# A trunk layer on one core: the output projection in seven block products for all tokens, adds moved to accumulating transfers, and norm one's scale and offset put on after the transposes

## The chip, the core and the metric

The kernel runs on one core of a Trainium2 chip. That core has TensorE (PE, matmuls into PSUM; PEld is its weight load), VectorE (DVE), ScalarE (ACT), GpSimd (POOL) and SyncE (SP), and 16 DMA engines. The metric is the device time of one execution in microseconds; the result of a kernel is the median over its runs.

## The reference

One post-norm transformer layer for 1024 tokens of width 1024, all in float32:

```python
h = x @ w_in                                     # q, k, v of branches A and B, two gates
y_a = chunk_band_attention(...) @ w_proj_a       # softmax over a band
y_b = stick_breaking_attention(...) @ w_proj_b
mix = (sigmoid(ga + b_gate_a) * y_a + sigmoid(gb + b_gate_b) * y_b) @ w_out
x = layer_norm(ALPHA * x + mix, ln1_g, ln1_b)
g, u = split(x @ w_ffn_in)
x = layer_norm(ALPHA * x + (silu(g) * u) @ w_ffn_out, ln2_g, ln2_b)
```

ALPHA is 2 to the power 0.25. The change touches everything from the gated projection of branch B to the FFN's second matmul.

## The kernel before

A float32 product of two matrices is computed from operands that are each split into a high and a low part in a matmul type (`split`, lines 109 and 110: ACT casts the high part, DVE subtracts to get the low one); one product is three matmuls (high by high, high by low, low by high), each 128 x 128 by 512. Large products are cut into two by two blocks and computed in the Winograd form: seven block products p = 1 to 7 over sums of blocks instead of eight.

The work is one long program; a scheduler puts each engine's instructions into an order from the order in which the code is written, and `keep_in_program_order` holds single ones in place. Within an engine instructions run in that order, so one that waits holds all behind it. Transfers are issued by SP and wait in its order as well; POOL issues none. Buffers come from pools by tag (`op`, `xt`, `kp`, `bw`, `gt`, `pt`, `yt`, and `qs`, `kh`, `kl`, `v` as a ring); a tile waits for the last use of the tile that had its slot. PSUM banks have tags too (`mm`, `sc`, `tr`, `pv`); the transposes use `tr`, of which there are three.

The stages around the change:

- Branch B's projection runs over eight channel blocks c, in the order 6, 7, 5, 4, 2, 3, 1, 0, in two token halves each. DVE multiplies the product by the gate gB and adds branch A's part mA (line 1146), which gives the merged branch m.
- The output projection takes m (as weights, 128 tokens at a time) and w_out. For the half of the tokens it goes by seven products, two token tiles each, 12 matmuls for each (line 1369); for token tiles 4 to 7 it goes plainly, in two column halves of 24 matmuls (lines 116 to 119). `take_in` (line 1348) adds each to ALPHA * x in `acc` on DVE.
- Norm one: DVE takes statistics (line 1183) and aggregates (1186), POOL raises the variance to the power -1/2 (1187), and DVE applies mean and scale g (1188), then 1/std and offset b (1191), over 128 x 1024.
- `x1_operands` transposes x1 in 128 x 128 pieces on PE (1209), ACT copies them out of PSUM (1219 for the first token half, 1229 for the second), and they are split; DVE forms the block sums that the FFN's seven products need (1247 to 1250).
- The FFN's first block of columns f = 0 goes plainly (`plain_half`), the 21 others in seven products (`run_pairs`, line 179). Their left sums `sl` are stored, and FFN-out (line 1512) loads them back; x1 is stored in `x_dr` and reloaded into `x` (line 1444), and `take_down` adds each FFN-out product to it on DVE (lines 1486 and 1489).

A product of the output projection, as it is written before:

```python
        for j in range(2):
            accs = by if p in (2, 5, 3) else bx
            ...
            take_in(t0 + j, cs, accs[j], scale)
            if p in (3, 4):
                norm_1(t0 + j)
```

## Time and profile before

| what | value |
|---|---|
| three runs | 1412.02, 1413.35, 1412.03 us (median 1412.03) |
| profiled execution | 1412.51 us, its span 1410.7 us |
| granted TensorE clock, mean | 0.999 |
| PE | 1399.7 us, 99% of the span, 6642 matmuls |
| DVE | 1034.1 us, 73%, 1671 instructions |
| ACT | 699.0 us, 50%, 1245 instructions |
| POOL | 236.0 us, 17%, 308 instructions |
| DMA | 292.28 MB, mean 207 GB/s |

Times in views are microseconds from the span's start. A row of the timeline or of the chain has start, length, engine, line, operation, output <- inputs, shapes and a count; in brackets stands how long the engine was idle before it and what released it. A row of groups has the count, the busy time and the mean in ns, and the idle time before. Rows on a transfer give how many, their size and the time from issue to landing.

### The profile page before, as it was taken

The page shows a single profiled execution, that of the slowest core. Times are in us where ns is not written, and L with a number is a line of the kernel's source. Part 1 is how long each engine was busy: PE and PEld are TensorE (multiplying, and loading weights), DVE is VectorE, ACT ScalarE, POOL GpSimd, SP SyncE. Part 2 cuts the span into 40 slices and gives each one's busy share as a digit, 9 for nine tenths or more (in the row PEclk, how much of TensorE's full clock was granted, in tenths as well). Part 3 has the DMA queues.
Part 4 walks back from the last instruction along what each step waited for, and adds up shares of the span by engine and source line. Part 5 has one row for each costly group of instructions (what it writes and reads, how often), then busy time and mean ns, then how long its engine had stood idle before and what let it go on. Part 6 is the DMA issues. An engine that isn't in the chain of part 4 may idle for free.

```text
span 1410.7 us, 18935 instructions
## 1 busy us (share of the span) xinstructions
PE 1399.7 (99%) x6642; PEld 1164.6 (83%) x6642; DVE 1034.1 (73%) x1671; ACT 699.0 (50%) x1245; POOL 236.0 (17%) x308
## 2 busy tenths in 40 slices
PE   9999999999999999999999999999999999999997
PEld 7888888888888888888888888888888888888886
DVE  8967657545887788878998967767677765847666
ACT  6544444545888888774413644434444443322220
POOL 0000000002555878750001000000000000000033
PEclk9999999999999999999999999999999999999999
DMA  7476468856676478755651144433444349996652
GB/s 254 165 286 224 178 236 303 295 179 238 212 231 208 130 252 281 253 198 194 231 202 75 61 148 166 149 141 143 164 164 149 143 144 342 411 385 236 233 194 90
DMA packets 98927, 292.28 MB, mean 207 GB/s; under 512 B 9728, under 2 KB 26112, under 8 KB 98832
## 3 DMA queue, kind: packets, MB, share of 16 engines
q1 hardware_dynamic: 98832, 291.07, 58.2%
q8 instruction: 52, 0.85, 0.3%
q14 instruction: 43, 0.35, 0.1%
HBM read 187.20 MB, written 100.17 MB: 204 GB/s over the span
## 4 chain that ended last, share of the span: by engine, by line
PE 94%; DVE 2%; DMA 1%; ACT 1%; issue 1%; POOL 0%; DVEq 0%; SPq 0%; ACTq 0%; POOLq 0%
PE sxf L179 16%; PE d L1512 15%; PE sxp L179 9%; PE szf L179 8%; PE v L481 5%; PE gps L606 4%; PE szp L179 4%; PE syf L179 4%; PE yAps L910 3%; PE ops L1369 3%; PE syp L179 2%; PE tp_b L817 2%; PE tp_a L817 2%; PE plain L347 1%; PE pv_b L833 1%; PE pv_b L832 1%
## 5 line engine op out<-in xcount | busy, mean ns | idle before, releaser
L1512 PE MATMUL d<-wd,sl 128*128 128x512 f32 (+1 forms) x924 | 207.7, 387 | 0.0
L1512 PEld LDWEIGHTS d<-wd,sl 128*128 128x128 f32 x924 | 172.3, 188 | 35.4
L1532 POOL TENSOR_TENSOR mv<-mv,neghalf 128x1 f32<-128x1 f32 x8 | 9.0, 1121 | 606.7 <-DVE mv L1531 606.7
L109 ACT CAST wd<-wd 128x512 fp32r<-128x512 f32 x77 | 45.9, 621 | 114.1 <-PE d L1512 66.8
L794 POOL TENSOR_TENSOR w_b<-w_b,kp_b 128x511 f32<-128x511 f32 (+3 forms) x96 | 96.0, 1012 | 23.2 <-DVE kp_b L789 16.7
L110 DVE TENSOR_TENSOR sl<-h,sl 128x512 fp32r<-128x512 f32 x77 | 52.6, 686 | 27.6 <-ACT sl L109 27.6
L789 DVE TENSOR_TENSOR_SCAN kp_b<-kp_b,ident_ps 128x512 f32<-128x512 f32 (+2 forms) x64 | 56.5, 885 | 21.0 <-ACT kp_b L786 20.0
L109 ACT CAST sl<-h 128x512 fp32r<-128x512 f32 x77 | 47.5, 620 | 48.1 <-PE syf L179 18.3
L1489 DVE TENSOR_TENSOR x<-d,x 128x512 f32<-128x512 f32 (+1 forms) x41 | 27.6, 675 | 47.6 <-PE d L1512 47.5
L786 ACT ACTIVATE kp_b<-sc_b 128x512 f32<-128x512 f32 (+3 forms) x96 | 48.3, 504 | 28.0 <-PE sc_b L706 23.6
L110 DVE TENSOR_TENSOR wd<-wd,wd 128x512 fp32r<-128x512 f32 x77 | 52.7, 709 | 10.7 <-ACT wd L109 10.6
L179 PE MATMUL szf<-x1S63h,wcf 128*128 128x512 f32 x168 | 55.1, 389 | 0.0
L110 DVE TENSOR_TENSOR pt_b<-tp_b,pt_b 128x512 fp32r<-128x512 f32 (+1 forms) x96 | 49.9, 544 | 6.6 <-ACT pt_b L109 5.7
...
L109 ACT CAST pt_b<-tp_b 128x512 fp32r<-128x512 f32 (+1 forms) x96 | 46.6, 503 | 8.0 <-PE tp_b L817 7.6
L759 POOL TENSOR_SCALAR w_a<-w_a,st_a 128x640 f32<-128x640 f32 (+2 forms) x64 | 42.2, 669 | 48.0 <-PE sc_a L706 26.6
L754 ACT ACTIVATE w_a<-w_a,st_a 128x640 f32<-128x640 f32 (+2 forms) x64 | 44.7, 700 | 8.6 <-DVE st_a L748 7.5
L787 ACT ACTIVATE w_b<-sc_b 128x511 f32<-128x511 f32 (+3 forms) x96 | 48.3, 504 | 0.0
L817 PE MATMUL tp_b<-ident,w_b 128*128 128x128 f32 x288 | 47.3, 272 | 0.2
L110 DVE TENSOR_TENSOR pt_a<-tp_a,pt_a 128x512 fp32r<-128x512 f32 (+1 forms) x96 | 44.6, 486 | 3.3 <-ACT pt_a L109 2.2
L1307 ACT ACTIVATE h<-sxf 128x512 f32<-128x512 f32 x21 | 12.6, 598 | 68.2 <-PE sxf L179 68.2
L817 PEld LDWEIGHTS tp_b<-ident,w_b 128*128 128x128 f32 x288 | 36.4, 140 | 11.1 <-DVE pt_b L110 1.1
...
## 6 DMA issues: line engine op xcount, KB each, us to landing
s_dr<-sl SPq DMA_DIRECT2D x77, 512.0 KB, 2.6
sl<-s_dr SPq DMA_DIRECT2D x77, 512.0 KB, 7.6
wLf<-in_w_ffn_in_dram SPq DMA_DIRECT2D x22, 512.0 KB, 4.3
wRf<-in_w_ffn_in_dram SPq DMA_DIRECT2D x22, 512.0 KB, 3.6
wd<-in_w_ffn_out_dram SPq DMA_DIRECT2D x22, 512.0 KB, 8.2
v_dr<-vc SPq DMA_DIRECT2D x16, 512.0 KB, 3.4
qs<-q_dr SPq DMA_DIRECT2D x16, 512.0 KB, 6.7
kh<-k_dr SPq DMA_DIRECT2D x16, 512.0 KB, 6.5
```

The lines of the kernel that those rows point to most:

```text
L109: return (nc.scalar.copy(dst_h, src), nc.vector.tensor_tensor(dst_l, src, dst_h.bitcast(F32), ALU.subtract))
L110: nc.vector.tensor_tensor(dst_l, src, dst_h.bitcast(F32), ALU.subtract))
L179: mm(acc, lw[:, ks], rx, start=(first and kt == i == 0), stop=(kt == 3 and i == 2), skip_group_check=not first)
L481: mm(accs[j], a, b, start=(first and kt == n == 0), stop=(kt == 3 and n == 2), skip_group_check=True)
L606: mm(acc[hf], lw[:, ks], rx[k][:, (LO, HI)[hf]], start=(k == j == 0), stop=(k == KT - 1 and j == 2))
L754: nc.scalar.activation(s[:, 0:w], s[:, 0:w], AF.Exp, bias=st[:, m:m + 1], scale=-1.0, accum_out=st[:, 2:3])
L786: nc.scalar.activation(kp[:, c0:e], sc[:, 0:n], AF.Sigmoid, scale=-1.0)
L787: nc.scalar.activation(be[:, m0:e], sc[:, m0 - c0:n], AF.Sigmoid)
L789: nc.vector.tensor_tensor_scan(kp[:, 0:e], kp[:, 0:e], ident_ps()[:, 0:e], 0.0, ALU.mult, ALU.add)
L794: nc.gpsimd.tensor_tensor(be[:, m0:e], be[:, m0:e], kp[:, m0 - 1:e - 1], ALU.mult)
L817: ins = tr(tp[:, (qb - lo_q) * P:(qb - lo_q + 1) * P], wt[qb - q0][:, (kb - qb) * P:(kb - qb + 1) * P], ident)
L1512: mm(part, a, b, start=(fresh and i == k == 0), stop=(i == n - 1 and k == 2), skip_group_check=not fresh)
```

## The change

*The output projection.* All eight token tiles go by seven products, four tiles each, in the order 1, 2, 5, 3, 6, then 7 and 4 interleaved by tile. That is 336 matmuls instead of 360. Products 1, 5 and 3 are evicted by ACT with 1/ALPHA, and x is added to them by a transfer that POOL issues and that accumulates into the tile; products 2, 6, 7 and 4 are added by DVE with 1/ALPHA. The norm is taken of x + mix/ALPHA, with EPS divided by ALPHA squared.

*Branch sums.* Branch A's part, and the left block sums `sum_1` and `sum_2`, are added by accumulating transfers from POOL. `sum_3` and `sum_4` stay on DVE. The left operands are split per product (`m_split`).

*Norm one.* POOL computes -mean/std with one more instruction, and ACT applies 1/std and it over 128 x 1024. Scale and offset are put on when x1 is evicted after its transposes, by columns of `gb_1`. `x_dr` keeps the norm without them; in FFN-out DVE multiplies by g (`scale_acc`), and POOL issues accumulating transfers that add b (`offset_acc`). `take_down` uses 1/ALPHA everywhere.

*Order.* Instructions of these stages are tied into lanes: "s" on ACT, "v" on DVE, "p" for POOL's transfers. FFN operands of f = 1 are formed during branch B, stored to DRAM by POOL and loaded back; those of f = 0 are loaded and split during the output projection. The sums of x1 are formed in two parts, later than before.

In counts: DVE has about 30 instructions fewer and ACT 20 more; POOL issues 45 transfers, where before it issued none.

```diff
+    lanes = dict(s=last_y[:1], v=last_y[1:])
+    def tied(lane, ins):
+        for before in lanes.get(lane, ()):
+            tc.add_manual_dep(ins.ins, before.ins.name, mybir.DependencyInfo(
+                mybir.DependencyClass.NoSync, mybir.DependencyReason.DATA), reason="lane")
+        lanes[lane] = [ins]
+        return ins
+    def halve(dst_h, dst_l, src):
+        hi, lo = split(dst_h, dst_l, src)
+        chain_s(hi)
+        chain(lo)
+    def plus(dst, src):
+        tied("p", nc.gpsimd.dma_start(dst, src, accum_op=ALU.add))
...
+    def sum_1(kt):
+        plus(m_raw[kt + 4][:, HI], m_raw[kt][:, HI])
+    def sum_2(kt):
+        plus(m_raw[kt][:, HI], m_raw[kt + 4][:, LO])
...
-            nc.vector.tensor_tensor(mA[:, cs], gB[:, cs], mA[:, cs], ALU.add)
+            chain(put(gB[:, cs], acc, gB[:, cs], ALU.mult))
+            if c < 2:
+                plus(gB[:, cs], m_dr[c][:, cs])
...
+    def statistics(name, n, tie=lambda ins: ins):
+        mv = sml.tile([P, 4], F32, name=f"mv{name}", tag="mv")
+        tie(nc.vector.bn_aggr(mv[:, 0:2], marks[name][:, 0:6 * n]))
         nc.gpsimd.tensor_tensor(mv[:, 2:3], mv[:, 1:2], neghalf, ALU.pow)
-        nc.vector.scalar_tensor_tensor(t, t, mv[:, 0:1], g, ALU.subtract, ALU.mult)
...
+    def scaled(dst, src, k):
+        chain_s(nc.scalar.activation(dst, src, AF.Identity, bias=gb_1[:, 8 + k:9 + k],
+                                     scale=gb_1[:, k:k + 1]))
...
+    def norm_1(tt):
+        mv, t = statistics(f"1_{tt}", 2, chain), acc_t[tt]
+        nc.gpsimd.tensor_scalar(mv[:, 3:4], mv[:, 0:1], mv[:, 2:3], -1.0, ALU.mult, ALU.mult)
+        chain_s(nc.scalar.activation(t, t, AF.Identity, bias=mv[:, 3:4], scale=mv[:, 2:3]))
...
+        if p in (1, 5, 3):
+            chain_s(nc.scalar.activation(t, accs[j], AF.Copy, scale=1 / ALPHA))
+            plus(t, x_rows(tt, cs))
+        else:
+            chain(nc.vector.scalar_tensor_tensor(t, accs[j], 1 / ALPHA, t, ALU.mult, ALU.add))
...
+    for n, (p, j) in enumerate(((7, 0), (7, 1), (4, 0), (7, 2), (4, 1), (7, 3), (4, 2), (4, 3))):
+        project_out(p, j)
+        if p == 4:
+            norm_1(j + 4)
+        if n > 3:
+            x1_operands(0, acc_t, (n - 4,))
...
+    def scale_acc(tts, cs):
+        for t in (acc_t[tt][:, cs] for tt in tts):
+            nc.vector.tensor_tensor(t, t, g1[:, cs], ALU.mult)
+    def offset_acc(tt):
+        nc.gpsimd.dma_start(acc_t[tt], bass.AP(tensor=ln1_b.tensor, offset=ln1_b.offset,
+                                               ap=[[0, P], [1, D]]), accum_op=ALU.add)
...
+    g1 = bcast(ln1_g, slot("xt", "ln1g"))
     load_acc(range(4))
+    scale_acc(range(4), LO)
```

Three places show how instructions move; a row has the line, the operation, output <- inputs, the shape, and in brackets the semaphores that it waits for. The first is ACT's order around the first evictions of x1 (`x1ps` are the transposed banks, `x1raw` their copies, `x1A` the operands, `acc` a token tile, `mv` its statistics). Before:

```order
L1219 COPY x1raw_7736<-x1ps_0_7726 128x512 [waits PE_49]
L1219 COPY x1raw_7736<-x1ps_4_7731 128x512 [waits PE_49]
L109 CAST x1A_0_7737<-x1raw_7736 128x512 [waits Activation_49]
L109 CAST x1A_0_7741<-x1raw_7736 128x512 [waits Activation_49]
L1219 COPY x1raw_7791<-x1ps_1_7781 128x512 [waits PE_49]
L1219 COPY x1raw_7791<-x1ps_5_7786 128x512 [waits PE_49]
L109 CAST x1A_1_7792<-x1raw_7791 128x512 [waits Activation_49]
L109 CAST x1A_1_7796<-x1raw_7791 128x512 [waits Activation_49]
```
Afterwards:

```order
L1399 ACTIVATE acc_7416<-acc_7416,mv_5_7787 128x1024 [waits DVE_49,Pool_49]
L1246 ACTIVATE x1raw_7802<-x1ps_0_7792,gb_7224 128x512 [waits PE_49]
L109 CAST x1A_0_7803<-x1raw_7802 128x512 [waits Activation_49]
L1246 ACTIVATE x1raw_7802<-x1ps_4_7797,gb_7224 128x512 [waits PE_49]
L109 CAST x1A_0_7807<-x1raw_7802 128x512 [waits Activation_49]
L1246 ACTIVATE x1raw_7837<-x1ps_1_7827,gb_7224 128x512 [waits PE_49]
L109 CAST x1A_1_7838<-x1raw_7837 128x512 [waits Activation_49]
L1246 ACTIVATE x1raw_7837<-x1ps_5_7832,gb_7224 128x512 [waits PE_49]
L109 CAST x1A_1_7842<-x1raw_7837 128x512 [waits Activation_49]
L1399 ACTIVATE acc_7418<-acc_7418,mv_6_7860 128x1024 [waits DVE_49,Pool_49]
L1246 ACTIVATE x1raw_7875<-x1ps_2_7865,gb_7224 128x512 [waits PE_49]
```
Norms of later token tiles (acc with mv_5 and mv_6) now stand on ACT ahead of and between the evictions, and each cast follows the copy it reads.

The second is DVE's order in the same place (`ops` are product banks, `bn` the statistics). Before:

```order
L110 TENSOR_TENSOR x1A_1_7792<-x1raw_7791,x1A_1_7792 128x512 [waits Activation_49]
L1188 SCALAR_TENSOR_TENSOR acc_7440<-acc_7440,mv_4_7772,ln1g 128x1024 [waits DVE_49]
L110 TENSOR_TENSOR x1A_1_7796<-x1raw_7791,x1A_1_7796 128x512 [waits Activation_49]
L1191 SCALAR_TENSOR_TENSOR acc_7440<-acc_7440,mv_4_7772,ln1b 128x1024 [waits DVE_49,Pool_49]
L110 TENSOR_TENSOR x1A_2_7811<-x1raw_7810,x1A_2_7811 128x512 [waits Activation_49]
L110 TENSOR_TENSOR x1A_2_7815<-x1raw_7810,x1A_2_7815 128x512 [waits Activation_49]
L1185 TENSOR_SCALAR bn_7_7936<-bn_7_7936 128x1
L1348 SCALAR_TENSOR_TENSOR acc_7442<-acc_7442,ops_1_7819 128x512 [waits PE_49]
```
Afterwards:

```order
L1421 SCALAR_TENSOR_TENSOR acc_7416<-ops_1_7265,acc_7416 128x512 [waits PE_49]
L1227 BN_STATS bn_5_7731<-acc_7416 128x6 [waits DVE_49]
L1235 BN_AGGR mv_5_7787<-bn_5_7731 128x2 [waits DVE_49,Pool_49]
L110 TENSOR_TENSOR x1A_0_7803<-x1raw_7802,x1A_0_7803 128x512 [waits Activation_49]
L110 TENSOR_TENSOR x1A_0_7807<-x1raw_7802,x1A_0_7807 128x512 [waits Activation_49]
L1421 SCALAR_TENSOR_TENSOR acc_7420<-ops_3_7312,acc_7420 128x512 [waits DMASW0_49,PE_49]
L1227 BN_STATS bn_7_7824<-acc_7420 128x6 [waits DVE_49]
L1229 TENSOR_SCALAR bn_7_7824<-bn_7_7824 128x1 [waits DVE_49]
L110 TENSOR_TENSOR x1A_1_7838<-x1raw_7837,x1A_1_7838 128x512 [waits Activation_49]
L110 TENSOR_TENSOR x1A_1_7842<-x1raw_7837,x1A_1_7842 128x512 [waits Activation_49]
L1421 SCALAR_TENSOR_TENSOR acc_7418<-ops_2_7290,acc_7418 128x512 [waits PE_49]
L1227 BN_STATS bn_6_7770<-acc_7418 128x6 [waits DVE_49]
```
The takes of the next products (lines 1421) stand behind the low halves of the operands (line 110), where both wait for ACT.

The third is DVE's order shortly before FFN-out's first matmul (`gt`, `h` are the FFN's tiles, `syf` and `sxf` its banks, `wd` FFN-out's weights). Before:

```order
L1304 TENSOR_TENSOR h_10893<-h_10893,gt_10840 128x512 [waits DVE_49]
L1308 TENSOR_TENSOR h_10893<-h_10893,gt_10840 128x512 [waits Activation_49]
L194 TENSOR_TENSOR gt_10977<-syf_10980,gt_10977 128x512 [waits PE_49,Activation_49]
L110 TENSOR_TENSOR wd_1_0_11104<-wd_0_11084,wd_1_0_11104 128x512 [waits DMAHW3_49,Activation_49]
L110 TENSOR_TENSOR wd_1_3_11113<-wd_3_11087,wd_1_3_11113 128x512 [waits DMAHW2_49,Activation_49]
L110 TENSOR_TENSOR wd_1_1_11107<-wd_1_11085,wd_1_1_11107 128x512 [waits DMAHW0_49,Activation_49]
L194 TENSOR_TENSOR gt_10977<-sxf_10964,gt_10977 128x512 [waits PE_49]
```
Afterwards:

```order
L1354 TENSOR_TENSOR h_10890<-h_10890,gt_10837 128x512 [waits DVE_49]
L1358 TENSOR_TENSOR h_10890<-h_10890,gt_10837 128x512 [waits Activation_49]
L1519 TENSOR_TENSOR x_0_11073<-x_0_11073,ln1g 128x512 [waits DMAHW6_49,DMAHW4_49,DMAHW2_49]
L197 TENSOR_TENSOR gt_10974<-syf_10977,gt_10974 128x512 [waits PE_49,Activation_49]
L1519 TENSOR_TENSOR x_1_11074<-x_1_11074,ln1g 128x512 [waits DMAHW7_49,DMAHW3_49]
L1519 TENSOR_TENSOR x_0_11073<-x_0_11073,ln1g 128x512
L1519 TENSOR_TENSOR x_1_11074<-x_1_11074,ln1g 128x512
L197 TENSOR_TENSOR gt_10974<-sxf_10961,gt_10974 128x512 [waits PE_49,Activation_49]
L110 TENSOR_TENSOR wd_1_0_11103<-wd_0_11083,wd_1_0_11103 128x512 [waits Activation_49]
```
Multiplies of x_0 and x_1 by ln1g, which wait for transfers, stand ahead of the takes of syf and sxf.

More of the change, by code (lines that the diff above doesn't have):

```diff
@@ L167, in product @@
     def product(acc, W, ops, p, first):
[L169 removed]
+        if "all" in W:
+            wh, wl = (W["all"][p][:, cs] for cs in (LO, HI))
+        elif p == 3:
             wh, wl = W["c"][:, LO], W["c"][:, HI]
@@ new lines, in hybrid_trunk_kernel, with wf_part, part @@
+    x_, z_, y_, u_ = (t[:, cs] for t in wf1 for cs in (LO, HI))
+    def wf_part(p, src, *terms):
+        if terms:
+            chain(put(src, *terms, sub))
+        o = slot("pt", f"wf_{p}", F32R)
+        halve(o[:, LO], o[:, HI], src)
+        tied("p", nc.gpsimd.dma_start(wf_dr[p - 1], o.bitcast(F32)))
+    def part(f, *args):
+        return lambda: f(*args)
+    f1 = {3: part(wf_part, 3, u_), 1: part(wf_part, 1, x_), 5: part(wf_part, 5, x_, y_, x_),
+          7: part(wf_part, 7, y_, y_, u_), 6: part(wf_part, 6, u_, u_, x_),
+          2: part(wf_part, 2, z_), 4: part(wf_part, 4, z_, z_, u_)}
@@ new lines, in hybrid_trunk_kernel @@
+    sum_2(2)
+    sum_1(1)
+    for p in OUT[:5]:
+        for j in range(4):
+            project_out(p, j)
+            for work in aside[p, j]:
+                work()
+            if p == 6:
+                norm_1(j)
+    for n, (p, j) in enumerate(((7, 0), (7, 1), (4, 0), (7, 2), (4, 1), (7, 3), (4, 2), (4, 3))):
+        project_out(p, j)
+        if p == 4:
+            norm_1(j + 4)
+        if n > 3:
+            x1_operands(0, acc_t, (n - 4,))
+        if n == 2:
+            with tc.issue_after(wo["last"].ins):
+                load_f1((1, 2), "op")
@@ L1422, in hybrid_trunk_kernel @@
+    for tt in range(4):
+        dma(x1_dr[tt], acc_t[tt])
+    load_f1((6, 5, 7, 4), "bw")
+    with tc.issue_after(wo["last"].ins), tc.issue_after(lanes["v"][0].ins):
+        left_f(2)
     first_h = []
```

464 lines of the change are left out of this document (219 added, 245 removed).

## Prediction

> **What bounds the kernel now.** I read the page first, for the busiest engine and the chain of waits; then a table of stretches, for the stages that the change touches; then the chain inside them.
>
> ```profile
> PE 1399.7 (99%) x6642; PEld 1164.6 (83%) x6642; DVE 1034.1 (73%) x1671; ACT 699.0 (50%) x1245; POOL 236.0 (17%) x308
> PE 94%; DVE 2%; DMA 1%; ACT 1%; issue 1%; POOL 0%; DVEq 0%; SPq 0%; ACTq 0%; POOLq 0%
> ```
>
> PE is busy for 99% of the span and carries 94% of the chain. The stretches, with columns PE, PEld, DVE, ACT and POOL busy, the granted clock, the DMA share and GB/s, are the gated branch-B projection (640 to 681.6), the out-projection (to about 766.7), the start of the FFN, the end of FFN-in, and two pieces of FFN-out:
>
> ```profile
> 640.00:681.60 41.60, 41.60 (x185) 34.46 (x184) 36.70 (x65) 19.42 (x33) 0.00 (x0) 1.00 0.58 206
> 681.60:720.00 38.40, 38.40 (x171) 31.80 (x170) 34.63 (x49) 16.26 (x18) 1.13 (x2) 1.00 0.75 260
> 720.00:765.00 45.00, 45.00 (x216) 37.59 (x215) 41.76 (x61) 12.94 (x21) 5.08 (x5) 1.00 0.30 106
> 765.00:800.00 35.00, 34.91 (x170) 28.58 (x168) 30.68 (x43) 19.88 (x31) 1.58 (x1) 1.00 0.13 46
> 1170.00:1193.00 23.00, 23.00 (x103) 19.06 (x102) 10.28 (x18) 7.79 (x14) 0.00 (x0) 1.00 0.97 364
> 1193.00:1210.00 17.00, 17.00 (x76) 14.08 (x76) 14.58 (x24) 6.32 (x12) 0.00 (x0) 1.00 0.94 361
> ```
>
> From 640 to 800 us PE is idle for 0.09 us. So matmuls that go there shorten the run one for one, and DVE, though 90% busy, is worth nothing as long as it keeps up: whatever it or ACT is freed of there lies under PE. What can be lost is a new wait of PE.
>
> **The change, part by part.**
>
> *Matmuls.* Before, four of the eight out-projection blocks go by seven products (7 x 2 x 12 = 168) and four plainly (4 x 2 x 24 = 192), 360 in all. Afterwards it is 7 x 4 x 12 = 336. The chain shows the 168 as one piece:
>
> ```profile
> 681.64 38.08 PE ops L1369 x168
> 747.82 1.77 PE x1ps L1209 x16
> 794.90 0.61 DVE h L1280
> 795.56 3.01 PE syf L179 x12
> ```
>
> 38.08 / 168 is 0.227 us for a matmul, so 24 fewer are **-5.44 us**. The transposes stay 64, at 1.77 / 16 = 0.11 us. The short break before 795.56, which the first-layer sums of x1 set, should go too, since a product that needs those sums comes later: -0.09 us, the whole of what PE lost there.
>
> *The end of the out-projection.* This is the new wait. Before, the transposes of token blocks 0 to 3 stood between plain matmuls, and their evictions were bare copies in pairs that depended on nothing later. Now the last three blocks' norms and those evictions are tied into one order on ACT and one on DVE (the lanes "s" and "v"): norm 5, four copy-and-cast pairs, norm 6, two pairs, norm 7, two pairs. A norm waits for its block's last matmul, for DVE's take, statistics and aggregate, for POOL's power and for a new POOL multiply; behind it on ACT wait the evictions, which hold the three transpose banks and feed the first FFN product. On DVE the next block's take waits behind the low halves of those same evictions. So the two orders alternate and cannot overlap. Their durations:
>
> ```profile
> 761.28 0.39 PE L116 MATMUL ops<-wh_o,mo 128*128 128x512 f32 x1
> 761.49 0.69 DVE L1348 SCALAR_TENSOR_TENSOR acc<-acc,ops 128x512 f32<-128x512 f32 x1 [0.39 <-PE ops L119]
> 762.93 0.21 DVE L1186 BATCH_NORM_AGGREGATE mv<-bn 128x2 f32<-128x12 f32 x1
> 722.75 0.55 POOL L1187 TENSOR_TENSOR mv<-mv,neghalf 128x1 f32<-128x1 f32 x1 [4.39 <-DVE mv L1186]
> 763.18 1.28 DVE L1188 SCALAR_TENSOR_TENSOR acc<-acc,mv,ln1g 128x1024 f32<-128x1024 f32 x1
> 763.29 1.58 POOL L1187 TENSOR_TENSOR mv<-mv,neghalf 128x1 f32<-128x1 f32 x1 [4.19 <-DVE mv L1186]
> L779 POOL MEMSET w_b<- 128x1 f32 x64 | 4.7, 98 | 0.6 <-PE tp_a L817 0.6
> L960 ACT ACTIVATE gB<-gB,bg 128x1024 f32<-128x1024 f32 x4 | 4.6, 1151 | 0.0
> L550 ACT CAST wh_ot<-wr_ot 128x1024 fp32r<-128x1024 f32 x8 | 8.4, 1053 | 10.3 <-PE ops L1369 5.7 <-DMA wr_ot<-wt_drt 3.3 <-DVE ma L110 1.1
> L1219 ACT COPY x1raw<-x1ps 128x512 f32<-128x512 f32 x8 | 4.3, 594 | 6.2 <-PE x1ps L1209 6.1
> L109 ACT CAST x1A<-x1raw 128x512 fp32r<-128x512 f32 x8 | 4.6, 636 | 0.0
> 772.80 1.08 ACT L1229 COPY x1low<-x1ps 128x512 f32<-128x512 f32 x2 [15.13 <-PE x1ps L1209]
> 774.80 1.09 ACT L1229 COPY x1low<-x1ps 128x512 f32<-128x512 f32 x2
> 775.04 0.70 DVE x1A L110
> ```
>
> The block's matmuls end at 761.28; POOL starts its power at 763.29, 2.0 us later, and needs 0.55 us: 2.56. (The 1.58 belongs to a power that ran while DVE worked on two operands in SBUF, at 763.18; in the new order DVE waits for ACT at that moment, so I take 0.55.) The POOL multiply is not in this trace: between the smallest POOL row, 0.1, and a second power, 0.55; a multiply of 128x1 has no function to evaluate, so 0.2. The norm over 128x1024: a cast takes 1.05 and the gate, with one per-partition operand, 1.15, so with two 1.05 to 1.25; I take 1.2. A pair of eviction and cast: packed as the old order had them 1.0 (two pairs from 772.80 to 774.80), in series 0.594 + 0.636 = 1.23, and with two per-partition operands at 0.1 each up to 1.43; now each cast waits for its own copy, so 1.3.
>
> Counted from the end of block 5's last matmul: 2.56 + 0.2 + 1.2 = 3.96 for norm 5; four pairs, 9.2; then a low half (0.7), 2.35 from the start of the take (761.49) to the end of the power, 0.2 and 1.2, so norm 6 at 13.6; two pairs, 16.2; the same 4.45 again, norm 7 at 20.7; two pairs and a low half, **24.0 us**. With all low ends (the low half at 0.6) it is 20.6, with all high ends 26.2. PE's work from that matmul to the one that needs the last low half is 79 matmuls and 32 transposes, 17.9 + 3.5 = 21.4 us. So PE loses **2.5 us, between 0 and 4.8**. It falls in pieces: at the fourth transposed bank (the bank's release), at the eighth, and at the first FFN product's last operand.
>
> The Trainium skill, page SBUF — State Buffer, section Who interferes with whom, says that a DVE instruction with two SBUF inputs holds up a GpSimd one that reads SBUF; the 0.55 and 1.58 rows bear it out. Were all three powers hit, the sum here would rise by 3 x 1.03 us.
>
> *Left sums, branches and x by transfers.* Adds and gate branches move from DVE to accumulating transfers that POOL issues, 45 in all with the stores of f1's operands. Nothing in this trace is issued that way, so their landing is bounded by loads and stores of SP's queue:
>
> ```profile
> s_dr<-sl SPq DMA_DIRECT2D x77, 512.0 KB, 2.6
> acc<-in_x_dram SPq DMA_DIRECT2D x6, 512.0 KB, 6.6
> DMA to landing us min/median/max: 6.6/10.0/10.5
> ```
>
> So 2.6 to 10.5 us (the last row is x's reload in FFN-out). Most of the new ones are half as large, at a DMA share of 0.58 to 0.75: I take 5. POOL waits in order, and DVE and ACT wait for them in order. The tightest chain starts when the last gate product is taken, 0.9 us (0.21 + 0.69) after branch B's last matmul: branch, then left sum, two transfers in series, then cast and low half (1.4), due at the fifth product's last operand, 105 matmuls or 23.8 us later. That allows (23.8 - 0.9 - 1.4) / 2 = 10.7 us each. So **0 us**, covered by the first two products; uncovered, 2 us for each us above 10.7.
>
> The Trainium skill, page DMA: Bandwidth & Descriptors, section Anatomy of one DMA, fits a GpSimd-issued transfer at 2.0 us plus its bytes over 436 GB/s; by it 256 KB land in 2.6 us. No run here shows it; the sum would be the same 0.
>
> *FFN-out.* Scale and offset return as 12 multiplies on DVE and eight accumulating transfers of the offset. The scale loads behind x 0 and x 1 on SP, in a slot freed where the first left operand was loaded, and DVE now waits for it before a take that ACT and then PE wait for.
>
> ```profile
> 1174.88 0.32 SPq L1456 DMA_DIRECT2D sl<-s_dr  x1
> sl<-s_dr SPq DMA_DIRECT2D x1, 512.0 KB, 4.7
> DMA to landing us min/median/max: 9.3/9.3/9.3
> 1179.71 0.69 DVE L194 TENSOR_TENSOR gt<-syf,gt 128x512 f32<-128x512 f32 x1 [4.19 <-PE syf L179]
> 1180.44 0.63 ACT L1302 ACTIVATE gt<-gt 128x512 f32<-128x512 f32 x1 [2.93 <-DVE gt L194]
> 1182.36 0.59 ACT L207 COPY h<-sxf 128x512 f32<-128x512 f32 x1 [1.29 <-PE sxf L179]
> 1184.88 0.39 PE L179 MATMUL sxf<-x1S75h,waf21h 128*128 128x512 f32 x1
> 1197.32 0.68 DVE L1486 SCALAR_TENSOR_TENSOR x<-x,d 128x512 f32<-128x512 f32 x1
> 1210.33 0.68 DVE L1489 TENSOR_TENSOR x<-d,x 128x512 f32<-128x512 f32 x1
> ```
>
> A load issued at 1174.88 landed in 4.7 us, at 1179.6 (the second 9.3 is the later load of norm two's scale, in a busy stretch). The scale must land by 1184.88 - 0.69 - 0.69 - 0.63 - 0.59 = 1182.3, 7.4 us after issue: **0 us** at 4.7, 1.9 us at 9.3. Four of the multiplies then fill DVE's idle time (10.28 busy of 23); the next four, 2.4 us, delay takes that have a step of 13 us to spare. An offset has from 1197.3 + 0.7 to 1210.3, 12.3 us, before it holds DVE, and about 10 more before its bank is wanted.
>
> *Sum.* -5.44 - 0.09 + 2.5 = -3.0 us. The profiled execution took 1412.51 us, 1.81 of them outside its span of 1410.7; it would take 1409.5. The runs' median, 1412.03, is 0.48 lower, so I predict **1409.0 us**.
>
> **The rivals.** (A) No new wait: the two orders keep up, all of the low ends. For it: PE's work reaches 21.4 and the low sum is 20.6; against it, a cast that must wait for its copy. 1406.5. (B) Slower: the accumulating transfers take 14 us because each reads and writes its target and they queue in order; from 10.7 us on the fifth product waits, here 2 x 3.3 = 6.6 us: 1415.6. For it: x's reload took 10.0; against it, that was at a DMA share of 0.94, twice the size. (C) The scale lands in 9.3 us: +1.9, 1410.9. For it: a share of 0.97 there; against it, the neighbour's 4.7. (D) The powers are slow after all: +3.1, 1412.1, no change. The first three powers of the old order, when DVE was less busy around them, argue against it.
>
> **How the numbers follow.** Forecast 0.46 (1406.5 to 1411.3 by the stall's ends), A 0.18, B 0.14, C 0.12, D 0.10. About 0.2% can be told from no change, 1409.2 and 1414.9. Faster: A and over half of the forecast, 0.43. Slower: B's upper part and combinations of B, C and D, 0.2. Same: the rest, 0.37. The range runs from 1405.8, A with the offset and sums gaining a little, to 1414.8, which leaves out B from about 13.5 us.
>
> **What would show it.** PE should count 24 matmuls fewer, at the same 0.227 us. In a window over the end of the out-projection PE should be idle for 2 to 3 us in three pieces, released by ACT; POOL's powers there should take 0.55. Between branch B's end and the sixth product PE should be idle for nearly nothing; an idle piece at the fifth product released by a transfer is B. An idle piece some 8 us before FFN-out's first matmul, released by ACT, is C. I am wrong if PE waits anywhere else by more than a microsecond, or if DVE's two-microsecond delay at FFN-out's start reaches PE.

## The result and the profile after

The changed kernel took 1433.29 us (median of 4 runs, 1432.45 to 1435.13), the kernel before beside it 1412.69 (1412.02 to 1414.06). The ratio is 1.0146, with a 95% interval of 1.0129 to 1.0164: 20.6 us slower, where 1409.0 was forecast and 1414.8 was the end of the range. The prediction is wrong in sign. Of all the executions behind the numbers below, one of run 11's ten took 6757 us; it moves that run's median from 1413.71 to 1414.11.

The page of the changed kernel, its engine line, its chain and its two main transfer queues (q1 is SP's, q0 is POOL's; packets, MB, share of 16 engines):

```profile
PE 1401.0 (98%) x6618; PEld 1161.6 (81%) x6618; DVE 1013.8 (71%) x1641; ACT 716.5 (50%) x1265; POOL 271.0 (19%) x361
PE 86%; DMA 5%; DVE 3%; ACT 2%; issue 2%; POOL 1%; SPq 0%; DVEq 0%; POOLq 0%; ACTq 0%
q1 hardware_dynamic: 98256, 287.41, 56.0%
q0 software_dynamic: 6480, 17.30, 5.9%
```

The 24 matmuls are gone (6642 to 6618), but PE's busy time did not fall by 5.44 us, it rose by 1.3; and PE, idle for 11.0 us of the old span, is idle for 1430.7 - 1401.0 = 29.7. That is the whole account of the 20.0 us between the two spans: -5.44 for matmuls, +18.7 of idle time, +6.7 of busy time beyond the matmuls' nominal 0.227 us each. The waits of PE (us in total, times, longest) name most of the idle time:

```profile
PE ops L1413 <- DVE gB L1197: 8.4, 1, 8.4
PE d L1588 <- DMA sl<-s_dr: 4.7, 1, 4.7
PE ops L1413 <- ACT m L109: 2.3, 2, 1.7
PE x1ps L1256 <- ACT x1raw L1246: 2.0, 2, 1.2
PE plainhl_0f L116 <- ACT x1A L109: 0.7, 1, 0.7
```

Together 18.1 us; before, none in these stages reached 0.3. The last two rows are the wait that the prediction put at 2.5 us. The first is where the kernel lost most. The timeline around it, of SP, DVE and PE:

```profile
676.85 0.38 SPq L1187 DMA_DIRECT2D gB<-g_dr  x1
674.58 0.69 DVE L1197 TENSOR_TENSOR gB<-yBps,gB 128x512 f32<-128x512 f32 x1 [4.33 <-DMA gB<-g_dr]
690.99 0.69 DVE L1197 TENSOR_TENSOR gB<-yBps,gB 128x512 f32<-128x512 f32 x1 [7.23 <-DMA gB<-g_dr]
692.93 0.80 PE L1413 MATMUL ops<-woh,m 128*128 128x512 f32 x1 [8.39 <-DVE gB L1197]
```

Branch B's last gate is loaded by SP, plainly. Issued at 676.85, it landed near 691, after 14 us. DVE, in its order, stood before the last two gate products for 7.2 us; the second of them frees the bank that the out-projection's second token tile needs; PE stood for 8.4. The chain of waits (start, us, what) runs through an accumulating left sum that landed at the same time, so two late transfers end together there; and its last row is what PE did next:

```profile
681.24 10.15 DMA gA<-gB
691.59 0.51 DVE m L110
692.19 0.70 DVE gB L1197
692.93 5.24 PE ops L1413 x12
```

The same kernel's windows (columns as in the prediction's table: PE, PEld, DVE, ACT, POOL busy, granted clock, DMA share, GB/s), with the first row from the kernel before:

```profile
640.00:692.00 52.00, 52.00 (x231) 43.07 (x230) 47.09 (x82) 25.82 (x40) 0.00 (x0) 1.00 0.60 209
```

```profile
640.00:692.00 52.00, 44.52 (x196) 36.26 (x194) 27.81 (x41) 17.79 (x25) 11.96 (x16) 0.96 0.95 287
660.00:680.00 20.00, 20.00 (x90) 16.57 (x89) 12.02 (x19) 5.76 (x8) 3.76 (x5) 1.00 1.04 336
688.00:692.00 4.00, 0.00 (x0) 0.00 (x0) 1.01 (x2) 0.58 (x1) 0.00 (x0) 0.50 1.07 308
692.00:696.00 4.00, 3.07 (x7) 2.51 (x8) 2.68 (x5) 0.03 (x1) 2.64 (x3) 0.50 1.04 372
```

The DMA engines went from a share of 0.60 to 0.95 and are full from 660 on (a row above 1 reads as full), while the bytes per second rose far less, from 209 to 287. And the granted clock is 0.50 at the wait's end and for some us after it: the 12 matmuls from 692.93 take 5.24 us in the chain for a nominal 2.72, so the wait costs 2.5 us more than its length. The Trainium skill, page TensorE: Matmul & The Clock Gate, section Part 1: The HAM clock gate (the "warmup" mystery), has the clock at half after an idle window of about 3.4 us until PE has been busy for about as long. The 0.50 rows agree with the first part; full speed came back at about 697.8, some 5 us after PE resumed (an estimate from the mean of 0.78 between 696 and 700).

The transfers of that stretch, 640 to 692 us, first of the kernel before, then of the change (queues with MB and share of 16 engines; issues with size and median us to landing):

```profile
q1 hardware_dynamic: 2979, 10.83, 59.5%
gB<-g_dr SPq DMA_DIRECT2D x4, 512.0 KB, 4.5
```

```profile
q0 software_dynamic: 2220, 7.46, 56.1%
q1 hardware_dynamic: 2254, 7.41, 39.1%
wf_dr<-wf POOLq DMA_DIRECT2D x7, 512.0 KB, 8.9
gB<-g_dr SPq DMA_DIRECT2D x5, 512.0 KB, 12.0
gA<-gB POOLq DMA_DIRECT2D x3, 512.0 KB, 10.8
gB<-m_dr POOLq DMA_DIRECT2D x3, 512.0 KB, 11.4
```

The plain gate load now takes 12.0 us in the median instead of 4.5. In FFN-out, 1190 to 1250 us, POOL's queue holds nothing but the offsets, which gives their price directly; again before, then after:

```profile
q1 hardware_dynamic: 6195, 22.55, 95.9%
```

```profile
q1 hardware_dynamic: 5182, 18.87, 81.1%
q0 software_dynamic: 576, 2.10, 17.8%
sl<-s_dr SPq DMA_DIRECT2D x23, 512.0 KB, 10.2
```

and PE's timeline in the changed kernel:

```profile
1237.56 7.72 PE L1588 MATMUL d<-wd,sl 128*128 128x512 f32 x27 [4.70 <-DMA sl<-s_dr]
```

The accumulating 2.10 MB held 17.8% of 60 us, 10.7 us of all 16 engines, or **5.1 us per MB**; SP's transfers beside them 48.7 us for 18.87 MB, 2.6 per MB. The engines were at 95.9% before, so there was no room for the offsets: in the same 60 us SP's queue moved 3.7 MB less. A left operand came late, PE waited 4.7 us, and the 27 matmuls behind it took 7.72 us instead of 27 x 0.227 = 6.13.

### The profile page after: what moved, and what is told of

It is laid out like the page before. It is cut to its first block, busy times and chain, and to the rows that moved or that the text cites. A ratio compares the mean times of both kernels' runs of the same rounds, so it can differ in the third digit from the quotient of the medians.

```text
span 1430.7 us, 19000 instructions
## 1 busy us (share of the span) xinstructions
PE 1401.0 (98%) x6618; PEld 1161.6 (81%) x6618; DVE 1013.8 (71%) x1641; ACT 716.5 (50%) x1265; POOL 271.0 (19%) x361
## 4 chain that ended last, share of the span: by engine, by line
PE 86%; DMA 5%; DVE 3%; ACT 2%; issue 2%; POOL 1%; SPq 0%; DVEq 0%; POOLq 0%; ACTq 0%
PE sxf L182 16%; PE d L1588 13%; PE sxp L182 9%; PE szf L182 8%; PE v L484 5%; PE szp L182 5%; PE gps L610 4%; PE syf L182 4%; PE yAps L914 3%; PE syp L182 2%; PE tp_b L821 2%; PE tp_a L821 2%; PE plain L350 1%; DMA sl<-s_dr 1%; PE pv_b L837 1%
## 5 line engine op out<-in xcount | busy, mean ns | idle before, releaser
L1522 POOL DMA_DIRECT2D x<-in_ln_b_dram x8 | 7.0, 872 | 465.8 <-DMA sl<-s_dr 426.2
L1413 PE MATMUL ops<-woh,m 128*128 128x512 f32 x224 | 72.8, 401 | 10.8 <-DVE gB L1197 8.4
L1564 DVE SCALAR_TENSOR_TENSOR x<-d,x 128x512 f32<-128x512 f32 (+1 forms) x57 | 38.5, 677 | 49.4 <-PE d L1588 49.4
L109 ACT CAST sl<-h 128x512 fp32r<-128x512 f32 x77 | 47.5, 620 | 46.6 <-PE syf L182 18.3
L1413 PEld LDWEIGHTS ops<-woh,m 128*128 128x128 f32 x224 | 43.1, 193 | 22.0 <-DVE gB L1197 8.8
L182 PE MATMUL szf<-x1S73h,wcf 128*128 128x512 f32 x160 | 52.5, 389 | 0.0
## 6 DMA issues: line engine op xcount, KB each, us to landing
sl<-s_dr SPq DMA_DIRECT2D x77, 512.0 KB, 10.1
wd<-in_w_ffn_out_dram SPq DMA_DIRECT2D x22, 512.0 KB, 10.1
```

The costliest lines, as they stand in the source:

```text
L109: return (nc.scalar.copy(dst_h, src), nc.vector.tensor_tensor(dst_l, src, dst_h.bitcast(F32), ALU.subtract))
L182: mm(acc, lw[:, ks], rx, start=(first and kt == i == 0), stop=(kt == 3 and i == 2), skip_group_check=not first)
L1413: mm(accs[j], a, b, start=(first and i == n == 0), stop=(i == 3 and n == 2), skip_group_check=not first)
```

## The experiments

Eighteen kernels ran (no run has the number 17). Each is compared with the kernel before on the same chip; "idle" and "slow" split the difference of the profiled span from that of before (1410.7) by PE's line on the page, besides the -5.44 us of matmuls that all share: idle is span less PE's busy time less 11.0, slow is busy time less 1394.3.

| run | median us | ratio to before | span | idle | slow |
|---|---|---|---|---|---|
| the change | 1433.29 | 1.0146 [1.0129, 1.0164] | 1430.7 | 18.7 | 6.7 |
| 1 plain writes | 1423.42 | 1.0077 [1.0062, 1.0093] | 1423.2 | 11.5 | 6.4 |
| 2 gate first | 1433.05 | 1.0144 [1.0129, 1.0159] | 1431.6 | 16.6 | 9.7 |
| 3 no offsets | 1426.35 | 1.0094 [1.0078, 1.0111] | 1426.1 | 15.4 | 5.4 |
| 4 small f = 1 stores | 1429.41 | 1.0118 [1.0098, 1.0139] | 1426.5 | 14.4 | 6.8 |
| 5 adds on DVE | 1426.90 | 1.0104 [1.0089, 1.0119] | 1425.9 | 12.5 | 8.1 |
| 6 offsets later | 1425.43 | 1.0093 [1.0078, 1.0108] | 1423.1 | 12.8 | 5.0 |
| 7 order at the end | 1433.27 | 1.0151 [1.0134, 1.0168] | 1430.6 | 18.3 | 7.0 |
| 8 = 5 + 6 + 7 | 1418.73 | 1.0047 [1.0032, 1.0062] | 1418.3 | 10.1 | 2.9 |
| 9 = 5 + 6 | 1422.25 | 1.0070 [1.0053, 1.0087] | 1420.9 | 8.7 | 6.9 |
| 10 = 9 + 2 | 1419.42 | 1.0047 [1.0032, 1.0062] | 1419.1 | 8.4 | 5.4 |
| 11 = 10 + 4 | 1414.11 | 1.0014 [1.0004, 1.0024] | 1411.9 | 4.2 | 2.4 |
| 12 = 10 + untied evictions | 1416.80 | 1.0029 [1.0017, 1.0041] | 1414.4 | 6.7 | 2.4 |
| 13 = 12 + early operands | 1416.97 | 1.0030 [1.0019, 1.0040] | 1416.3 | 6.7 | 4.3 |
| 14 = 13 + plain branch | 1410.68 | 0.9994 [0.9984, 1.0003] | 1408.1 | 2.4 | 0.4 |
| 15 = 13 + branch on POOL | 1418.27 | 1.0035 [1.0021, 1.0049] | 1417.3 | 7.6 | 4.4 |
| 16 = 15 + later split | 1417.70 | 1.0035 [1.0022, 1.0047] | 1415.9 | 7.3 | 3.3 |
| 18 branch on DVE | 1413.62 | 1.0012 [1.0003, 1.0021] | 1411.1 | 4.6 | 1.2 |
| 19 branch and sums on DVE | 1412.74 | 1.0004 [0.9996, 1.0013] | 1412.6 | 4.6 | 2.7 |

### Is it the accumulating?

Run 1 issues the same transfers of the same bytes from the same places, but none of `plus` accumulates:

```diff
-        tied("p", nc.gpsimd.dma_start(dst, src, accum_op=ALU.add))
+        tied("p", nc.gpsimd.dma_start(dst, src))
```

> The 30 transfers of the lane p that POOL issues for the branches, the left sums and x write plainly instead of accumulating (so the branches, sums and x are left out of the result); every engine's order stays as it is, and bytes and queue too. Theory A (an accumulating transfer holds the DMA engines about twice as long as its bytes, and this fills them from 660 to 725 us): the gate loads land in 5 to 8 us instead of 12 to 14, PE's 8.4 us wait before the second product tile shrinks below 2 us and the slow clock behind it goes; 1433.3 falls by 9 to 13 us, to about 1422. Theory B (the order on SP: the two loads of f0's weights hold the last gate's load in front of them) and theory C (it is the bytes and the software queue as such, whatever the transfer does): the wait stays above 6 us and the time within 3 us of 1433.

Measured 1423.42, 9.9 us less than the change, with the 8.4-us wait gone. Its transfers from 640 to 692 us:

```profile
q1 hardware_dynamic: 2864, 9.38, 50.1%
q0 software_dynamic: 2397, 8.57, 41.4%
gB<-g_dr SPq DMA_DIRECT2D x5, 512.0 KB, 9.0
```

POOL's queue moves 8.57 MB in 41.4% of 52 us, 2.5 us per MB. In the change it is f = 1's seven plain stores (3.67 MB, 9.2 us at that rate) and 3.79 MB that accumulate in the remaining 20.0 of 29.2 us: 5.3 per MB, about twice. So an accumulating transfer costs the DMA engines here what two plain ones do. Who issued the transfers stayed as it was and so is not the cause. POOL's time to issue one did not stay: it fell from 0.87 to 0.54 us, about 10 us over the 30. But the load that PE waited for is SP's, and POOL was busy for only 12.0 of the 52 us in the change, so this time is not what held it.

The gate loads landed in 9.0 us, later than the 5 to 8 of theory A. Nor did the slow clock shrink (6.4 against 6.7): behind the gate it is gone, but in this run a wait of 1.7 us at product 7 lowered the clock too, to 0.50 from 744 to 746.

Run 2 is the rival that SP's order alone makes the gate late: two weight loads of the FFN stood ahead of the last gate load.

```diff
-        dma(gB, g_dr[2 * c + 1])
+        last_gate = dma(gB, g_dr[2 * c + 1])
...
+    with tc.issue_after(last_gate.ins):
         for t, n in ((L0, 0), (R0, NF)):
```

> The two loads of f0's weights stand behind the last gate's load on SP; nothing else moves. Theory B: the last gate's load starts at about 671 us, when its slot is freed, instead of 676.9, PE's 8.4 us wait shrinks to under 2.5 us, and the time falls by 7 to 10 us, to about 1425. Theory A alone: the DMA engines are full all the same and the other gates (issued at 662) land at 674.6 as before, DVE's order is late by that, and the wait shrinks by less than 3 us; 1430 to 1433.

The gate was issued 5.8 us earlier, at 671.10, and the time did not move: the wait for the gate fell to 2.6 us, but ops waited 3.9 for ACT's m (2.3 in the change) and 2.1 for DVE's acc, and PE lost 3.0 us more to the slow clock. (The wait of 4.7 for `sl` is one of 4.2 for DVE's wd in the same place.) With the engines full, the order here only chose who waits.

Run 3 leaves the offsets out, run 6 issues them later, and run 4 shortens f = 1's stores:

```diff
-            if s in (0, 2):
-                offset_acc(j + 2 * s)
+            if s in (8, 9):
+                offset_acc(j + 4 * (s - 8))
```

```diff
-        tied("p", nc.gpsimd.dma_start(wf_dr[p - 1], o.bitcast(F32)))
+        cols = slice(0, 1024 if p == 3 else 64)
+        tied("p", nc.gpsimd.dma_start(wf_dr[p - 1][:, cols], o[:, cols].bitcast(F32)))
```

> The eight accumulating transfers of norm one's offset in FFN-out are left out (so the offset is missing on the residual path). If they are what lets the left operands' loads come late at 1232 us: PE's 4.7 us wait there goes, with some 1.8 us of slow clock behind it, and the time falls by 5 to 7 us, to about 1427. Rival (the multiplies by the scale, which put 12 more operations into DVE's order, or x's loads, make it late): the wait stays above 3 us and the time within 2 us of 1433.

> The eight accumulating transfers of the offset start in FFN-out's ninth and tenth steps instead of its first and third, where the DMA engines are busy for 66% instead of 100%; the result is whole. Theory (their place in a full stretch makes the left operands late): PE's 4.7 us wait at 1232 goes and no other comes, 5 to 7 us less, about 1427, as in the run without them. Rival (they cost the same wherever they are): a wait of 3 us or more after 1315 us, 1430 or more.

> Six of the seven stores of f1's operands write 64 columns instead of 1024 (and f1's products all use the third operand, so its result is not the right one): 3 MB less in plain transfers on POOL's queue during branch B, no accumulate touched. Theory C (bytes on the software queue): the gates land in under 9 us, PE's 8.4 us wait shrinks below 3, the time falls by 6 to 11 us. Theory A: the stores end by about 665 and the wait shrinks by less than half, 1428 to 1432. Theory B: within 2 us of 1433.

Without offsets 6.9 us less, with late offsets, which leave nothing out, 7.9 less; in both the 4.7-us wait for `sl` is gone. So the offsets' price is all in whom they displace. Behind the last left operands they displace nothing that PE waits for; only DVE's statistics of norm two wait for them there, 10.7 us. The small stores gave 3.9 us, which is theory A's time, and cut the gate wait from 8.4 to 2.8, which is theory C's wait: plain traffic in the same stretch counts too.

### Taking the accumulating transfers away, and the order at the end

Run 5 puts the left sums, x and branch sums of the kept blocks back on DVE; run 7 moves the transposes two tiles ahead and product 7's left operands to the first two tiles of product 6; run 8 does all three edits, run 9 leaves the order of run 7 out again, and run 10 adds run 2's.

```diff
-        plus(m_raw[kt + 4][:, HI], m_raw[kt][:, HI])
+        t = m_raw[kt + 4][:, HI]
+        chain(put(t, t, m_raw[kt][:, HI], ALU.add))
...
-        if p in (1, 5, 3):
-            chain_s(nc.scalar.activation(t, accs[j], AF.Copy, scale=1 / ALPHA))
-            plus(t, x_rows(tt, cs))
-        else:
-            chain(nc.vector.scalar_tensor_tensor(t, accs[j], 1 / ALPHA, t, ALU.mult, ALU.add))
+        chain(nc.vector.scalar_tensor_tensor(t, accs[j], 1 / ALPHA, t, ALU.mult, ALU.add))
```

```diff
-        if n > 3:
-            x1_operands(0, acc_t, (n - 4,))
+        if 1 < n < 6:
+            x1_operands(0, acc_t, (n - 2,))
...
-        (6, 0): [part(m_split, 7, 2)],
-        (6, 1): [part(m_split, 7, 3)],
-        (6, 2): [part(m_split, 7, 1)],
-        (6, 3): [part(m_split, 7, 0), part(wo_split, 4, 1), part(wo_split, 4, 0)]}
+        (6, 0): [part(m_split, 7, 2), part(m_split, 7, 3)],
+        (6, 1): [part(m_split, 7, 1), part(m_split, 7, 0)],
+        (6, 2): [],
+        (6, 3): [part(wo_split, 4, 1), part(wo_split, 4, 0)]}
```

> Of the accumulating transfers before FFN-out only the five loads of branch A's part (seven transfers) stay: the three additions of gated branches to kept tiles, the eight left sums go back to DVE, x is loaded plainly into its tile, and DVE takes products 1, 5 and 3 as it takes the others. Theory A (accumulating transfers hold the DMA engines twice as long as plain ones): the software queue's share from 640 to 692 us falls from 56% to about 40%, the gates land in under 10 us, PE's 8.4 us wait falls below 2, and the time falls by 8 to 12 us, to about 1423, about as in the run with plain writes. Rival (DVE's order, which now carries 31 more operations, becomes what PE waits for): a new wait of PE on DVE of over 4 us in the output projection, and 1428 or more.

> At the output projection's end the evictions of the transposed blocks are written two products earlier, ahead of norms 5 to 7 on ACT, and product 7's four left operands are split after the first two tiles of product 6 instead of one after each. If norms that stand ahead of them on ACT cost what the trace shows there: the waits on those operands (2.3 us), on the evictions (2.0) and on the last operand (0.7) shrink to under 2 us together, and the time falls by 2 to 4 us, to about 1430. Rival (the transposes now wait for norms 0 to 3 instead, or the evictions for each other): the waits stay at 4 us or more and the time within 1 us of 1433.

> The three edits together: adds on DVE, offsets later, the earlier evictions. If their gains add up (10, 6.5 and 3 us): about 1413.5, between 1410 and 1417, that is within 0.3% of the kernel before. If what is left of the waits is one and the same thing seen three times: 1418 or more. Below 1411 only if the 24 matmuls' 5.4 us come through nearly whole.

> The two parts that helped alone, together, in the change's own order at the out-projection's end: left sums, x and the branch sum added by DVE as before (x loaded plainly), and the eight offsets issued when the left operands of FFN-out's last products have been loaded. Alone they took 6.4 and 7.9 us off the changed kernel's 1433.3. Theory (two separate stretches, each lost to accumulating transfers): the gains add, 1433.3 - 14.3 = 1419.0, between 1417.5 and 1420.5. Rival (the reordered transposes of the run with all three edits cost or gave something): more than 1.5 us away from that run's 1418.7.

> The same, and SP issues the two weight loads of the FFN's first columns behind branch B's last gate load instead of ahead of it. With all three edits the last gate load was still issued late, at 671.88, and took 14.4 us; PE then waited 3.7 us at the first product's second token tile and ran on a lower granted clock after it. Theory A (the transfers fill the engines, so order only moves the wait, as it did when this edit was made alone: 1433.05): 1419 within 1.5. Theory B (with the adds on DVE there is room, and the order now counts): the 3.7 us and 1 to 1.5 us of low clock go, 1414.0 within 1.0.

Run 5 gave 6.4 us, less than the 8 to 12 expected: the gate wait fell to 3.6, not below 2. Run 7 gave nothing, its rival: its wait for ACT's m fell to 0.2 us, but one of 1.6 for DVE's takes and one of 1.6 for ACT's norm came in its place. Run 8 gave 14.6 us, not the 19.5 expected; that is what runs 5, 6 and 7 gave alone, 6.4 + 7.9 + 0.0. Run 9 missed its expectation by 3 us. Its idle time is less than run 8's; what it has more of is slow clock, 6.9 against 2.9, and in its window from 740 to 760 the granted clock is 0.91 where run 8 has 1.00. Runs 8 and 9 were on different chips, and run 9's times lie 4 us apart, so I do not rank them. Run 10's 1419.42 is theory A's: the gate wait went from 3.7 to 1.6, not to nothing, the one for ACT's m grew from 1.7 to 2.9, and one of 1.3 at an FFN product is new.

Runs 11 and 12 take more from the stretch and from the end: run 11 has run 4's small stores, and run 12 leaves x1's evictions and splits out of the lanes, so that ACT has both evictions of a pair ahead of the next norm.

```diff
-        chain_s(nc.scalar.activation(dst, src, AF.Identity, bias=gb_1[:, 8 + k:9 + k],
-                                     scale=gb_1[:, k:k + 1]))
+        nc.scalar.activation(dst, src, AF.Identity, bias=gb_1[:, 8 + k:9 + k],
+                             scale=gb_1[:, k:k + 1])
...
-                    halve(o[:, LO], o[:, HI], part)
+                    split(o[:, LO], o[:, HI], part)
```

> The same as the one before, and six of the seven stores of the f = 1 operands write 64 of 1024 columns (loads read the third operand each time), so 2.8 MB less is written on POOL's queue; the result is not the reference's for f = 1's columns. Alone the small stores took 3.9 us off. Theory A (the DMA engines are still full until the gate has landed): 3 to 4 us less than the run before. Theory B (the run before has no wait left there): within 1 us of it.

> As the run with the gate loads first, and at the out-projection's end the evictions of the transposed x1 and their splits are not tied to ACT's and DVE's lanes, so that both evictions of a pair stand next to each other and ahead of the norm of a later token tile. The changed kernel waits there 2.7 us for evictions and casts, as predicted, and 2.3 us for the left operands of product 7, which are tied behind norms. Theory (the tie sets the waits for evictions): 2 to 3 us less than the run with gate loads first. Rival (the work of two engines in turn is too long in any order, as when the transposes were moved ahead without gain): within 0.7 us of it.

Run 11 is 5.3 us below run 10, more than either theory gave; 4.2 us of the two spans' difference are idle time and 3.0 slow clock. No wait is left between branch B and product 6. What remains is the end of the out-projection, as in the change:

```profile
PE x1ps L1258 <- ACT x1raw L1248: 2.1, 2, 1.2
PE ops L1416 <- ACT m L109: 1.7, 1, 1.7
PE plainhl_0f L116 <- ACT x1A L109: 0.7, 1, 0.7
```

In run 12 the two waits for evictions are one of 1.1 us, so the tie did cost about 1.7 us, though the wait for ACT's m grew by 0.9. The medians are 2.6 apart, with intervals that overlap; the two spans differ by 4.7, of which 3.0 are slow clock, and that the edit made this part is not shown. Run 13 then moves product 7's left operands as run 7 did, and run 14 also lets the seven transfers of branch A's part write plainly:

```diff
-                plus(gB[:, cs], m_dr[c][:, cs])
+                tied("p", nc.gpsimd.dma_start(gB[:, cs], m_dr[c][:, cs]))
...
-                plus(gB, m_dr[c])
+                tied("p", nc.gpsimd.dma_start(gB, m_dr[c]))
```

> As the run with untied evictions (1416.8), and product 7's four left operands are formed two each in the first two tiles of product 6, ahead of norms 1 and 2, instead of one in each tile behind a norm. There PE waited 3.8 us in two pieces at the first products of that kind, released by ACT's cast of the operand. Theory (the order on the two lanes sets that wait): it goes, 1413.2 within 1.0, and the wait named ACT m is under 0.5 us. Rival (lateness handed down: the operand's cast and subtraction are late whatever stands ahead): within 1 us of 1416.8.

> The same as the run before, and the seven transfers of branch A's part (gB from m_dr, 2.5 MB) write without accumulating, so branch B's part is left out of the merged branch and the result is not the reference's. Theory (an accumulating transfer holds the DMA engines about twice as long per byte): the transfers land in 5 to 8 us instead of 10.7, PE's remaining 1.7 us at the gate product goes, 1 to 2 us less than the run before. Rival (the wait is set by the gate loads' buffers): the same time within 0.7.

Run 13's rival held: the wait for m (3.8 us in run 12) is gone and PE waits 3.6 us for DVE's take instead. Run 14 is 6.3 us below it, over three times what was expected: not only the gate's wait went, the one at product 6's end shrank too, and little clock was lost. First run 13's waits of 1 us and more in these stages, then run 14's:

```profile
PE ops L1415 <- DVE acc L1419: 3.6, 1, 3.6
PE ops L1415 <- DVE gB L1198: 1.6, 1, 1.6
PE plainhl_0f L116 <- ACT x1A L109: 1.0, 1, 1.0
```

```profile
PE ops L1415 <- DVE acc L1419: 1.7, 1, 1.7
PE plainhl_0f L116 <- ACT x1A L109: 1.1, 1, 1.1
```

Run 14's span, 1408.1, is 2.6 us below that of before: the matmuls' -5.44 with 2.4 of idle time and 0.4 of slow clock. That is near the forecast's sum (-3.0), in a kernel in which nothing accumulates ahead of FFN-out. But it is the fastest of ten executions; by the medians run 14 is 1.6 us below before, with an interval that includes no change. And the likeness is in part luck: the wait of 1.7 us for DVE's take is not one that the forecast had.

### Can it be had whole?

Run 14 leaves branch B's part out. The last runs load branch A's part plainly into slots (`pt`) that f = 1's operands have left. Run 15 adds it on POOL, run 16 also splits product 4's right operands later, run 18 adds it on DVE with the left sums by transfer as in the change, run 19 has both on DVE:

```diff
+        if c not in kept:
+            mA = slot("pt", f"mA{c}")
+            dma(mA, m_dr[c])
...
-            if c < 2:
-                plus(gB[:, cs], m_dr[c][:, cs])
+            if c not in kept:
+                tied("p", nc.gpsimd.tensor_tensor(gB[:, cs], gB[:, cs], mA[:, cs], ALU.add))
...
-            if c > 1:
-                plus(gB, m_dr[c])
```

> As the run with early operands (1416.97), with branch A's part of the five blocks loaded plainly by SP into slots that f = 1's operands have left, and added by ten POOL instructions of 128x512; no accumulating transfer is left before FFN-out, and the whole result is computed. POOL's rows for such an add are 1.29 us, against 7.4 and 10.8 us to the landing of an accumulating transfer. Theory (accumulating transfers fill the DMA engines): the 1.6 us at the gate product goes and lateness behind it too, 1411.5 within 1.5, close to the run with plain writes (1410.68). Rival (POOL's adds, slowed by DVE, are late as well, or the loads fill the engines as much): within 1.5 us of 1416.97.

> The same, and the two splits of product 4's right operands stand behind the first two tiles of product 7 instead of at the end of product 6, where they (2.4 us on DVE, 2.0 on ACT) stood ahead of the takes that PE waited 3.6 us for. Theory (order on the two lanes sets that wait): 1.5 to 3.5 us less than the run before, which would bring it to before or below. Rival (the wait moves again, to product 4's first tile): within 0.7 us of it.

> As the run with later splits (1417.70), branch A's part of the five blocks added by ten DVE instructions of 128x512 (0.68 us each) instead of POOL's, and the left sums 1 and 2 by eight accumulating transfers of 256 KB as in the change; x is added by DVE. DVE's work from 660 to 700 us is then about 35.2 (busy in the run with plain writes) + 6.8 for branch A - 4 for six or so of the sums, 38 of 40 us, without POOL's hindrance; the DMA engines have a share of about 0.5 when the sums are transferred. Theory (the loss is accumulating transfers before branch B's end and, with POOL, DVE's stretched rows): PE's waits at the gate products go, 1411.0 within 1.5. Rival (DVE is too full by now, or the sums land late): a wait of 2 us or more at a gate product or at the fifth product, 1414 or more.

> The same with the left sums on DVE too, so that no transfer before FFN-out accumulates: DVE's work from 660 to 700 us is 35.2 + 6.8 = 42 us, 2 more than there are. Theory (DVE becomes the bound): 1 to 3 us more than the run before, with PE waiting for DVE at the gate products or the first takes. Rival (what does not fit slides under the products behind 700 us, where DVE has 3 us to spare in 20): within 0.7 us of it.

Run 15's rival held. The DMA share from 680 to 700 fell from 0.76 to 0.46, but DVE is busy for 38.0 of the 40 us from 660 to 700, where run 13 had 30.8. Groups of DVE's instructions in that window, run 13 and then run 15, there with POOL's adds (busy us, mean ns):

```profile
L1198 DVE TENSOR_TENSOR gB<-yBps,gB 128x512 f32<-128x512 f32 x10 | 6.8, 683 | 0.2 <-PE yBps L119 0.2
L110 DVE TENSOR_TENSOR m<-gB,m 128x512 fp32r<-128x512 f32 x9 | 5.9, 683 | 4.5 <-ACT m L109 4.5
L1132 DVE TENSOR_TENSOR gA<-gA 128x512 f32<-128x512 f32 x3 | 2.1, 685 | 0.0
```

```profile
L1201 DVE TENSOR_TENSOR gB<-yBps,gB 128x512 f32<-128x512 f32 x10 | 6.8, 679 | 0.0
L110 DVE TENSOR_TENSOR m<-gB,m 128x512 fp32r<-128x512 f32 x9 | 8.6, 977 | 0.0
L1132 DVE TENSOR_TENSOR gA<-gA 128x512 f32<-128x512 f32 x3 | 5.3, 1782 | 0.0
L1203 POOL TENSOR_TENSOR gB<-gB,mA 128x512 f32<-128x512 f32 x10 | 17.5, 1762 | 9.2 <-DVE gB L1201 7.8 <-DMA mA<-m_dr 1.4
```

DVE's rows with both inputs in SBUF grew from 0.68 to 0.98 and 1.78 us, those that read a bank not at all. The Trainium skill, page SBUF — State Buffer, section Who interferes with whom, says that such a DVE instruction contends with a GpSimd one that reads SBUF; the rows agree, and show that both pay here: POOL's adds took 1.76 us in the mean, where its other rows of 128x512 take 1.29. Run 16 gave 0.6 us, its rival. Run 18, 1413.62, lies in neither expectation: waits of 2.3 us (in two pieces) for DVE at the gate, 1.5 for splits of weights and 1.1 at the end. Run 19, 1412.74, is 0.9 us below run 18, so the theory (1 to 3 us more) falls and the rival's 0.7 is just missed, with DVE busy for 19.9 of 20 us from 680 to 700 and PE waiting 2.5 us for it. Run 19 is no slower than before by what can be measured, and no faster. No version that computes everything beat the kernel before: the 5.44 us of matmuls are paid back at the gate, the weights' splits and the end, and in run 19 also in a wait of 1.4 us at an FFN product.

## Why the prediction was wrong, step by step

- **Matmuls, -5.44 us: right.** 24 fewer; the nominal 0.227 us holds wherever the granted clock is 1.00.
- **The end of the out-projection, +2.5 us: right in size and place.** Measured 2.0 + 0.7, in the three pieces named, released by ACT. POOL's power took 0.55 and its new multiply 0.27 (0.2 taken), the norm 1.24 (1.2), an eviction 0.77 and its cast 0.62, one pair following the other after 1.33 (1.3). Rivals A and D fall with it. (The low ends add up to 20.5, not 20.6, which changes nothing.) Run 12 shows that the tie made most of it: without it 1.1 us is left.
- **Missed beside it, +2.3 us:** product 7's left operands, tied behind norms 0 to 3. The step counted the norms 5 to 7 only. Runs 7 and 13 show that this wait is not that order alone: moved away, it came back at the take.
- **Accumulating transfers, "0 us, covered by the first two products": the step that failed, for about 11 us** (8.4 of wait and 2.5 of slow clock; run 1, without accumulating, was 9.9 us faster). The landing times were 8.1 to 11.4 us, about twice the 5 taken and near the bound of 10.5, but rival B's wait at the fifth product did not come. What failed is the question. I asked when each transfer's own reader needs it, and not what else uses the same engines. A share of 0.60 left room for 0.40 x 52 = 21 us of transfer time between 640 and 692 (the prediction quoted 0.58 and 0.75 for its two stretches); the change put 29.2 us on POOL's queue there and took 10.6 away from SP's (59.5% to 39.1% of 52 us). Even at the plain rate, POOL's 7.46 MB would have been 18.7 us, and run 4 and run 11 show that plain stores count. The victim is SP's gate load, then DVE in its order, then the bank, then PE.
- **FFN-out, scale: right.** `ln1g` was issued at 1187.31 and landed in 4.4 us; DVE stood 3.8 us for it, and PE did not wait. Rival C falls.
- **FFN-out, offsets, "12.3 us before it holds DVE, and about 10 more": the same failure again, for 6.3 us** (4.7 and 1.6). The offsets themselves were in time. The share of 0.97 and 0.94 was quoted for another purpose, and said that nothing more could be moved there without something else coming late.
- **What is not placed:** of the 6.7 us of busy time beyond nominal, 2.5 and 1.6 stand behind the two long waits; the other 2.6, and 0.6 of idle time, lie in pieces too small to name.

Runs 1, 3, 6 and 14 show the mechanism; that the accumulate's double price is a read and a write of its target was argued by rival B, and is not shown.
